# A hybrid decoder layer on one core: attention outputs split into high and low parts where they are made, and a second share of filling ahead of the last values

## The chip, the cores and the metric

The kernel runs on one core of one Trainium2 chip, as one program. The metric is the device time of one execution in microseconds (us). Engines go by their names in the profile: PE (TensorE, with PEld for its weight loads), DVE (VectorE), ACT (ScalarE), POOL (GpSimd), and SP, the engine whose queue issues nearly all transfers (DMA). Each engine works through its own instructions in order and waits on semaphores for the others.

## The reference

One layer over 1024 tokens of width 1024, all in float32: a half feed-forward, two gated attentions in parallel, a second half feed-forward, and a gated embedding. The change lies in the attentions and in the product that follows them.

```python
x = x + 0.5 * swiglu(rms_norm(x, ffn1_norm), ffn1_w_gate, ffn1_w_up, ffn1_w_down)
h = rms_norm(x, mix_norm)
fq, fk, fv, f_logit, sq, sk, sv, g_fox, g_sb = split_columns(h @ w_in)
...
y_fox = forgetting_attention(fq, fk, fv, log_f)       # 8 heads of 64, causal softmax
y_sb = stick_breaking_attention(sq, sk, sv)           # 8 heads of 64
merged = (sigmoid(g_fox) * (y_fox @ w_branch_fox)
          + sigmoid(g_sb) * (y_sb @ w_branch_sb))
x = x + merged @ w_out
x = x + 0.5 * swiglu(rms_norm(x, ffn2_norm), ffn2_w_gate, ffn2_w_up, ffn2_w_down)
x = x + sigmoid(rms_norm(x, ple_norm) @ w_ple_gate) * (p @ w_ple_proj)
```

Stick-breaking weights are `sigmoid(z[t,s])` times the product of `1 - sigmoid(z[t,j])` over the keys between s and t; the kernel makes these products with scans.

## The kernel before

**Split operands.** To multiply in float32 precision with a faster matmul type, the kernel splits an operand a into a high part (a rounded to that type, fp32r) and a low part (a minus the high part). A product is then three matmuls: high by high, high by low, low by high. `split` (lines 104 to 106) makes the two: a copy on ACT (L105), a subtraction on DVE (L106). Weights come in as RAW (L119) and are split into WH on ACT (L129) and WL on POOL (L139).

**Stages.** Feed-forward, then the projections of the attentions, then attention (about 850 to 1400 us of the profile), then the branch products, the output product, and the second feed-forward and embedding. In attention, 16 heads run one behind the other: heads 0 to 7 forgetting ("fox"), 8 to 15 stick-breaking. Two heads share a tile Y of 128 rows (64 each) by 1024 tokens, so there are eight pairs of heads, with two Y buffers.

**One step.** A head has four steps c = 0 to 3 of 256 queries each. `scores` makes the weights of a step: query-key matmuls (L1050, L1051), then for fox a sum and an exponential, for stick-breaking two sigmoids on ACT (L1058, L1059), scans on DVE (L1013, over tiles GF and RN) and multiplications on POOL (L1082). `apply` handles a step two steps later: for each pair of key blocks (`kpair` from c down to 0), PE transposes the weights (L1109), ACT copies the high part into a PT tile (L1111), DVE subtracts for the low part (L1117), and PE multiplies by the values (`values`, L1135). Values run two pairs behind the transposes; at a step's end come `values(1)`, a share of filling, and `values(0)`. The result is copied to Y by ACT (L1160) and added by DVE (L1163); the addition is issued late, at the next row of scores (`late`, `flush`).

**Filling.** PE has other work to put between: projections and stacking of later heads (L799, L807), in the last head the first branch products (L1396, gated by L1402). `fill[h]` lists the units of head h. Each call of `take`, which is what `fill` is in `scores` and `apply`, releases matmuls until their cost reaches a running target: the head's total, times the step's `share`, divided by the number of calls in that step. Some stacking units pause, and then a call gives nothing.

**The pair's way to the next product.** When the second head of a pair has its last step, SP stores the pair's Y to DRAM (`y_pairs`, L1167). In heads 14 and 15 `load_y` reads the pairs back, four at a time, into an X buffer, and `split_y` splits them with L105 and L106 on 128x1024 into H buffers, which the branch products (`branch_steps`, L1396) read as `yT[g][b]`: g is 0 for fox and 1 for stick-breaking, b is 0 for high and 1 for low. The table `Y_AT` says at which head and step the splits and loads stand. The last pair stays on the chip and is split at the end of `attention`.

**What sets the order.** The order on each engine comes from the order of the code, with a scheduler that places by dependence and by buffers: each tag (X, H, PT, Y ...) has a fixed number of them (PT has 4, H 4, X 2), and a new tile waits until the buffer's last user is done. For the stick-breaking heads `order("act", ...)` and `order("dve", ...)` pin ACT's and DVE's instructions to the order of the code. SP's transfers are one queue: one that waits holds up those behind it.

Of the kernel before, what the change touches and what calls it, by code (L numbers as in the profile page):

```python
# [10 lines left out]
F32 = mybir.dt.float32  # L11
# [7 lines left out]
P = 128  # L19
# [17 lines left out]
def tile_hybrid_decoder_layer(  # L37
# [119 lines left out]

    xd = dp.tile([S, D], F32, name="x_mid")
    pd = dp.tile([S, D], F32, name="p_proj")
    yd = dp.tile([8, P, S], F32, name="y_pairs")  # L160
    gd = dp.tile([16, P, S], F32, name="gates")
    fd = dp.tile([NH, S], F32, name="forget_sums")
    ad = [dp.tile([NF, P, 7, 512], F32, name=f"hidden_{i}") for i in range(2)]
# [930 lines left out]
    def apply(step, fill):  # L1094
# [58 lines left out]
        if c:  # L1153
            values(1)
        fill()
        values(0)
        Y = step["y"]
        hh = step["head"] % 2
# [3 lines left out]
        def add():  # L1162
            ins = nc.vector.tensor_add(ys, av[0:HD, :256], ys)  # L1163
            if not step["fox"]:
                order("dve", ins)
            if hh == 1 and c == 3 and step["last"] is False:
                nc.sync.dma_start(yd[Y["idx"]], Y["t"][:])  # L1167
        late.append(add)

    FOX_PAIRS = [2, 3, 0, 1]  # L1170
# [80 lines left out]
    def attention():  # L1251
# [26 lines left out]
        def any_bank():  # L1278
# [30 lines left out]
                s12 + g14[:1],  # L1309
                g14[1:] + s13,  # L1310
                s14 + g15[:1],
                g15[1:] + s15,
                fox_branch[:5]]

        fbs = [{} for _ in range(8)]
# [9 lines left out]
        for h in range(16):  # L1325
            fox = h < 8
            if h % 2 == 0:
                idx = fox_pairs[h // 2] if fox else 4 + (h - 8) // 2
                ys[h // 2] = {"t": slot("Y", [P, S]), "idx": idx}
            head = ys[h // 2]["idx"] % 4 * 2 + h % 2  # L1330
            v = (vf1, vf0, vs0, vs1)[h // 4]
            load_fb(h + 1)
            total = sum(u[0] for u in fill[h])
            state = [0.0, 0.0, 0]
            share = (0.27, 0.19, 0.27, 0.27)
            gens = [u[1] for u in fill[h]]

            def take(last=False):
                state[0] += total * share[state[2]] / (6, 7, 4, 5)[state[2]]
                while gens and (last or state[1] < state[0]):  # L1340
                    cost = next(gens[0], None)
                    if cost is None:
                        gens.pop(0)
                    else:
                        state[1] += cost
            for c in range(4):
                y0, y1 = Y_AT.get((h, c), ((), ()))
                split_y(*y0)
                load_y(*y1)
                step = {"fox": fox, "c": c, "head": head, "st": stacks[h], "v": v, "y": ys[h // 2], "last": h == 15, "id": 4 * h + c}  # L1350
                if fox:
                    step["fb"] = fbs[h]
                state[2] = c
                rows = scores(step, take)
                turns = apply(prev.pop(0), take) if len(prev) == 2 else iter(())
                next(rows)
                run(islice(turns, (1, 2, 1, 1)[c]))
                run(rows)
                run(turns)
                prev.append(step)  # L1360
            take(True)
# [9 lines left out]

    yT = []
    A = []
    Y_AT = {(14, 0): ((), range(4)), (14, 3): ((0, 1), (4, 5)), (15, 0): ((2, 3), (6,)), (15, 1): ((4, 5, 6), ())}

    Y_ = {}

    def load_y(*ks):
        for k in ks:
            if k == 0:  # L1380
                Y_["t"] = slot("X", [P, 4, S])
            nc.sync.dma_start(Y_["t"][:, k % 4, :], yd[k])

    def split_y(*ks):
        for k in ks:
            g, i = divmod(k, 4)
            if i == 0:
                yT.append((slot("H", [P, 4, S], F32R), slot("H", [P, 4, S], F32R)))
            hi, lo = yT[g]
            split(hi[:, i, :], lo[:, i, :], Y_["t"][:, i, :], nc.scalar, nc.vector, True)  # L1390

    def branch_steps(ps, g, m, half, w):
        i = 0
# [280 lines left out]
```

## Time and profile before

| | us |
|---|---|
| median of 3 runs | 2273.96 (2273.6 to 2276.03) |
| the profiled execution's own time | 2275.51 |
| its span in the trace | 2273.8 |
| PE busy in the span | 2241.4 |
| PE busy in 850 to 1400, of 550 us | 530.96 |
| DVE busy there | 378.09 |
| ACT busy there | 327.11 |
| POOL busy there | 336.32 |

The span runs from the first to the last instruction of the program; the execution's own time has the start and end around it as well. Busy times leave out waits and the issue of transfers. A row of the timeline reads: start, duration, engine, line, operation, output and inputs, shape, how many instructions; in brackets stands the idle time before them and what ended it.

### The profile page before, as it was taken

The page shows a single profiled execution, that of the slowest core. Times are in us where ns is not written, and L with a number is a line of the kernel's source. Part 1 is how long each engine was busy: PE and PEld are TensorE (multiplying, and loading weights), DVE is VectorE, ACT ScalarE, POOL GpSimd, SP SyncE. Part 2 cuts the span into 40 slices and gives each one's busy share as a digit, 9 for nine tenths or more (in the row PEclk, how much of TensorE's full clock was granted, in tenths as well). Part 3 has the DMA queues.
Part 4 walks back from the last instruction along what each step waited for, and adds up shares of the span by engine and source line. Part 5 has one row for each costly group of instructions (what it writes and reads, how often), then busy time and mean ns, then how long its engine had stood idle before and what let it go on. Part 6 is the DMA issues. An engine that isn't in the chain of part 4 may idle for free.

```text
span 2273.8 us, 30750 instructions
## 1 busy us (share of the span) xinstructions
PE 2241.4 (99%) x11402; PEld 1905.0 (84%) x11402; DVE 1490.0 (66%) x2296; ACT 1000.1 (44%) x1787; POOL 806.5 (35%) x803
## 2 busy tenths in 40 slices
PE   8999999999999999999999989999999999999999
PEld 6888888888888899989898878888888888888887
DVE  8845454688877326556578786789655555778753
ACT  6333333343455445565666663246333333434431
POOL 1444444300011236565467664410544444200121
PEclk9999999999999999999999999999999999999999
DMA  4232323474233343233223345732423232756132
GB/s 139 102 116 93 116 92 117 163 291 171 84 130 130 112 128 90 72 103 80 70 56 89 102 153 182 265 123 66 139 84 125 83 126 80 262 195 216 62 103 83
DMA packets 184904, 283.89 MB, mean 125 GB/s; under 512 B 27945, under 2 KB 104105, under 8 KB 184754
## 3 DMA queue, kind: packets, MB, share of 16 engines
q1 hardware_dynamic: 184752, 281.92, 37.4%
q8 instruction: 90, 1.47, 0.3%
q14 instruction: 60, 0.49, 0.1%
q10 hardware_dynamic: 2, 0.00, 0.0%
HBM read 189.83 MB, written 75.27 MB: 117 GB/s over the span
## 4 chain that ended last, share of the span: by engine, by line
PE 91%; DVE 5%; ACT 2%; issue 1%; DMA 0%; POOL 0%; SPq 0%; ACTq 0%; DVEq 0%
PE ps L556 39%; PE ps L454 21%; PE ps L799 8%; PE ps L807 4%; PE ps L1591 4%; PE ps L1396 3%; PE ps L1135 3%; PE ps L1109 2%; PE ps L506 2%; PE ps L1051 1%; PE ps L1050 1%; PE ps L956 1%; PE ps L228 1%; DVE PT L1117 1%; DVE RN L1013 1%
## 5 line engine op out<-in xcount | busy, mean ns | idle before, releaser
L454 PE MATMUL ps<-H,H 128*128 128x512 f32 x2184 | 497.7, 389 | 1.2 <-DVE X L462 1.2
L454 PEld LDWEIGHTS ps<-H,H 128*128 128x128 f32 x2184 | 409.3, 188 | 86.7 <-issue 2.0
L556 PE MATMUL ps<-H,WL 128*128 128x512 f32 x1116 | 265.0, 389 | 0.8 <-ACT WL L105 0.8
L556 PEld LDWEIGHTS ps<-H,WL 128*128 128x128 f32 x1116 | 209.4, 188 | 44.7 <-ACT WL L105 1.2
L556 PE MATMUL ps<-H,Q 128*128 128x512 f32 x612 | 146.0, 389 | 0.0
L462 DVE SCALAR_TENSOR_TENSOR X<-ps,X 128x512 f32<-128x512 f32 x168 | 109.0, 685 | 50.9 <-PE ps L454 50.9
L556 PEld LDWEIGHTS ps<-H,Q 128*128 128x128 f32 x612 | 114.9, 188 | 23.9
L556 PE MATMUL ps<-X,WL 128*128 128x512 f32 x552 | 132.6, 389 | 0.0
L1117 DVE TENSOR_TENSOR PT<-ps,PT 128x512 fp32r<-128x512 f32 (+1 forms) x160 | 100.3, 628 | 39.7 <-ACT PT L1111 38.4
L139 POOL TENSOR_TENSOR WL<-RAW,WH 128x512 fp32r<-128x512 f32 (+1 forms) x84 | 98.7, 1198 | 65.9 <-ACT WH L129 46.6
L556 PEld LDWEIGHTS ps<-X,WL 128*128 128x128 f32 x552 | 103.6, 188 | 21.5
L799 PE MATMUL ps<-WH,H 128*128 128x256 f32 x768 | 115.1, 288 | 0.6 <-ACT PT L962 0.3
L807 PE MATMUL ps<-H,WH 128*128 128x512 f32 x384 | 114.3, 408 | 0.6 <-ACT PT L926 0.6
L1135 PE MATMUL ps<-PT,X 128*128 128x256 f32 (+1 forms) x640 | 105.0, 290 | 9.5 <-DVE PT L1117 5.4
L219 POOL TENSOR_SCALAR ss<-ss 128x1 f32<-128x1 f32 x28 | 8.4, 299 | 297.9 <-ACT WL L215 232.8
L1111 ACT CAST PT<-ps 128x512 fp32r<-128x512 f32 (+1 forms) x160 | 87.6, 548 | 55.8 <-PE ps L1109 55.2
L1135 PEld LDWEIGHTS ps<-PT,X 128*128 128x128 f32 x640 | 91.8, 193 | 22.3 <-DVE PT L1117 11.3
L556 PE MATMUL ps<-H,PT 128*128 128x512 f32 x456 | 108.9, 389 | 0.0
L799 PEld LDWEIGHTS ps<-WH,H 128*128 128x128 f32 x768 | 101.0, 190 | 1.7 <-ACT PT L962 0.5
L556 PEld LDWEIGHTS ps<-H,PT 128*128 128x128 f32 x456 | 85.5, 188 | 17.8
L355 POOL TENSOR_TENSOR PT<-GF,RN 128x512 f32<-128x512 f32 x20 | 33.6, 1680 | 184.7 <-DVE GF L710 184.7
L1063 POOL TENSOR_TENSOR T<-T,l 128x128 f32<-128x128 f32 (+3 forms) x64 | 73.5, 1150 | 72.1 <-DVE l L1062 70.2
(431 smaller groups left out, 4899.1 us busy)
## 6 DMA issues: line engine op xcount, KB each, us to landing
hidden<-PT SPq DMA_DIRECT2D x40, 512.0 KB, 3.1
WH<-in_ffn_w_gate_dram SPq DMA_DIRECT2D x38, 512.0 KB, 5.5
Q<-hidden SPq DMA_DIRECT2D x24, 512.0 KB, 6.4
hidden<-RN SPq DMA_DIRECT2D x22, 512.0 KB, 2.6
KH<-in_ffn_w_up_dram SPq DMA_DIRECT2D x20, 512.0 KB, 6.4
KL<-in_ffn_w_up_dram SPq DMA_DIRECT2D x20, 512.0 KB, 6.9
T<-in_ffn_w_down_dram SPq DMA_DIRECT2D x20, 512.0 KB, 7.5
X<-in_x_dram SPq DMA_DIRECT2D x16, 512.0 KB, 9.8
```

The costliest lines, as they stand in the source:

```text
L139: ins = eng_lo.tensor_sub(lo[part], raw[part], f(hi[part]))
L454: pe(nc.tensor.matmul(groups[g][t][:], act[:, a, k, t * P:(t + 1) * P], wt[:, b, k, :], start=(fresh and n == 0), stop=(i in (6, 1, 4) and ...
L462: nc.vector.scalar_tensor_tensor(xs, groups[g][t][:], scale, xs, ALU.mult, ALU.add)
L556: pe(nc.tensor.matmul(ps[:], hl[:, a, k, :], rhs(m, b, k), start=(first and i == 0), stop=(final and i == 11), skip_group_check=True))
L799: pe(nc.tensor.matmul(ps[:, :n], hT[t // 4](a, k)[:, (t % 4) * P:(t % 4 + 1) * P], w[k // 4][b][:, k % 4, :n], start=(i == 0), stop=(i == ...
L807: pe(nc.tensor.matmul(ps[:], w[a][:, k, :], hT[half](b, k), start=(i == 0), stop=(i == 23)))
L1063: nc.gpsimd.tensor_mul(T[:, :n], T[:, :n], l[:].broadcast_to([P, n]))
L1111: high = nc.scalar.copy(pt[:, 0, :width], ps[:, :width])
L1117: ins = nc.vector.tensor_sub(pt[:, 1, :width], ps[:, :width], f(pt[:, 0, :width]))
L1135: pe(nc.tensor.matmul(o, lh, r, start=(kpair == c and i == 0), stop=(kpair == 0 and i == 3)))
L1396: pe(nc.tensor.matmul(ps[:], w[a][:, k, :], yT[g][b][:, k, half * 512:half * 512 + 512], start=(i == 0), stop=(i == 11)))
L1591: pe(nc.tensor.matmul(ps, hT[t // 4](a, k)[:, (t % 4) * P:(t % 4 + 1) * P], pl["w"][d, k // 2][b][:, k % 2, cs], start=(i == 0), stop=(i = ...
```

## The change

The tile `yd` in DRAM holds each pair twice, high and low. Each half of a pair (512 tokens, done after steps 1 and 3 of the second head) is split behind its addition: the high part goes into a PT tile by ACT, the low part is written over Y by DVE, and SP stores both. The loads in heads 13 to 15 bring the parts straight into the tiles that the products read; `split_y` is gone. `values(0)` has two calls of filling ahead of it, and the divisors of the shares follow. The units of head 14 are put in another order, with the last gate unit ahead of most of the last stacking.

```diff
-    yd = dp.tile([8, P, S], F32, name="y_pairs")
+    yd = dp.tile([8, 2, P, S], F32, name="y_pairs")
...
         if c:
             values(1)
         fill()
+        fill()
         values(0)
...
             ins = nc.vector.tensor_add(ys, av[0:HD, :256], ys)
             if not step["fox"]:
                 order("dve", ins)
-            if hh == 1 and c == 3 and step["last"] is False:
-                nc.sync.dma_start(yd[Y["idx"]], Y["t"][:])
+            if hh == 1 and c % 2 and not step["last"]:
+                cs = slice(c // 2 * 512, c // 2 * 512 + 512)
+                hi = slot("PT", [P, 512], F32R)
+                a = nc.scalar.copy(hi[:], Y["t"][:, cs])
+                b = nc.vector.tensor_sub(Y["t"][:, cs].bitcast(F32R), Y["t"][:, cs], f(hi[:]))
+                if not step["fox"]:
+                    order("act", a)
+                    order("dve", b)
+                nc.sync.dma_start(yd[Y["idx"], 0][:, cs], f(hi[:]))
+                nc.sync.dma_start(yd[Y["idx"], 1][:, cs], Y["t"][:, cs])
...
-                g15[1:] + s15,
+                s15[:1] + g15[1:] + s15[1:],
...
-                state[0] += total * share[state[2]] / (6, 7, 4, 5)[state[2]]
+                state[0] += total * share[state[2]] / (7, 8, 5, 6)[state[2]]
...
-                y0, y1 = Y_AT.get((h, c), ((), ()))
-                split_y(*y0)
-                load_y(*y1)
+                load_y(*Y_AT.get((h, c), ()))
...
-    Y_AT = {(14, 0): ((), range(4)), (14, 3): ((0, 1), (4, 5)), (15, 0): ((2, 3), (6,)), (15, 1): ((4, 5, 6), ())}
-
-    Y_ = {}
-
-    def load_y(*ks):
+    Y_AT = {(13, 0): (0, 0, range(4)), (14, 2): (0, 1, range(4)), (15, 0): (1, 0, range(4, 6)), (15, 1): (1, 1, range(4, 6)), (15, 2): (1, 0, (6,)), (15, 3): (1, 1, (6,))}
+
+    def load_y(g=None, b=None, ks=()):
+        if g is None:
+            return
+        if len(yT) == g:
+            yT.append([None, None])
+        if yT[g][b] is None:
+            yT[g][b] = slot("H" if g or b else "X", [P, 4, S], F32R)
         for k in ks:
-            if k == 0:
-                Y_["t"] = slot("X", [P, 4, S])
-            nc.sync.dma_start(Y_["t"][:, k % 4, :], yd[k])
-
-    def split_y(*ks):
-        for k in ks:
-            g, i = divmod(k, 4)
-            if i == 0:
-                yT.append((slot("H", [P, 4, S], F32R), slot("H", [P, 4, S], F32R)))
-            hi, lo = yT[g]
-            split(hi[:, i, :], lo[:, i, :], Y_["t"][:, i, :], nc.scalar, nc.vector, True)
+            nc.sync.dma_start(f(yT[g][b][:, k % 4, :]), yd[k, b])
```

In the changed kernel the lines from 1157 on are numbered one higher, then more: the addition is L1164, the new copy L1170, the new subtraction L1171, the stores L1175 and L1176, the loads L1391, the branch products L1397 and their gating L1403.

How the instructions move is shown at three places. First DVE's order in head 15, from the first gated branch product (into Q) to the next low part (PT) of `apply`, before:

```order
L1402 TENSOR_TENSOR Q_12688<-Q_12688,ps_12689 128x512
L106 TENSOR_TENSOR H_12771<-X_12300,H_12770 128x1024 x3
L1013 TENSOR_SCALAR GF_12681<-GF_12681,mask_sb 128x127
L1163 TENSOR_TENSOR Y_12299<-ps_12700,Y_12299 64x256
L1013 TENSOR_SCALAR RN_12716<-RN_12716,mask_sb 128x128
L1013 TENSOR_SCALAR RN_12716<-RN_12716 128x127
L1117 TENSOR_TENSOR PT_12795<-ps_12791,PT_12795 128x384
```

and with the change:

```order
L1403 TENSOR_TENSOR Q_12746<-Q_12746,ps_12747 128x512
L1117 TENSOR_TENSOR PT_12800<-ps_12795,PT_12800 128x512
L1013 TENSOR_SCALAR GF_12739<-GF_12739,mask_sb 128x127
L1164 TENSOR_TENSOR Y_12358<-ps_12758,Y_12358 64x256
L1013 TENSOR_SCALAR RN_12773<-RN_12773,mask_sb 128x128
L1013 TENSOR_SCALAR RN_12773<-RN_12773 128x127
L1117 TENSOR_TENSOR PT_12848<-ps_12844,PT_12848 128x384
```

Three splits of y pairs stood between the gating and the next scans and low parts; now none do.

Second DVE's order where the first half of the pair of heads 10 and 11 is complete (Y is the pair's tile, GF and RN are scans of the running step), before:

```order
L1013 TENSOR_SCALAR RN_11528<-RN_11528 128x256
L1163 TENSOR_TENSOR Y_10800<-ps_11509,Y_10800 64x256
L1013 TENSOR_SCALAR GF_11493<-GF_11493 128x256
L1117 TENSOR_TENSOR PT_11600<-ps_11596,PT_11600 128x384
L1013 TENSOR_SCALAR RN_11528<-RN_11528 128x256
```

and with the change:

```order
L1013 TENSOR_SCALAR RN_11572<-RN_11572 128x256
L1164 TENSOR_TENSOR Y_10836<-ps_11553,Y_10836 64x256
L1171 TENSOR_TENSOR Y_10836<-Y_10836,PT_11627 128x512
L1013 TENSOR_SCALAR GF_11538<-GF_11538 128x256
L1117 TENSOR_TENSOR PT_11649<-ps_11645,PT_11649 128x384
L1013 TENSOR_SCALAR RN_11572<-RN_11572 128x256
```

The subtraction stands directly behind the addition whose result it needs, and reads the PT tile that ACT fills in between; the scans and the low part stand behind it. The other thirteen halves look the same.

Third PE's order at the end of a step of head 14 (the values of `kpair` 1, branch products, the values of `kpair` 0, the next scores), before:

```order
L1135 MATMUL ps_12700<-PT_12731,X_10264 128x256 x4
L1396 MATMUL ps_12751<-H_12571,WL_12435 128x512
L1396 MATMUL ps_12751<-H_12571,WH_12433 128x512
L1396 MATMUL ps_12751<-H_12572,WH_12433 128x512
L1135 MATMUL ps_12700<-PT_12743,X_10264 128x256 x4
L1050 MATMUL ps_12783<-KH_12439,Q_12438 128x384
```

and with the change:

```order
L1135 MATMUL ps_12758<-PT_12787,X_10300 128x256 x4
L1397 MATMUL ps_12817<-X_11989,WH_12379 128x512
L1397 MATMUL ps_12817<-H_12562,WH_12379 128x512
L1397 MATMUL ps_12817<-X_11989,WL_12381 128x512
L1397 MATMUL ps_12817<-X_11989,WH_12379 128x512
L1397 MATMUL ps_12817<-H_12562,WH_12379 128x512
L1135 MATMUL ps_12758<-PT_12800,X_10300 128x256 x4
L1050 MATMUL ps_12836<-KH_12385,Q_12384 128x384
```

Five matmuls of filling stand between the two groups of values instead of three; the high part of y is now read from an X tile. In the first part of the stick-breaking heads two become four or three become six.

## Prediction

> **What bounds the kernel now.** I read first the shares of the whole page, then the chain that ended last.
>
> ```profile
> span 2273.8 us, 30750 instructions
> PE 2241.4 (99%) x11402; PEld 1905.0 (84%) x11402; DVE 1490.0 (66%) x2296; ACT 1000.1 (44%) x1787; POOL 806.5 (35%) x803
> PE 91%; DVE 5%; ACT 2%; issue 1%; DMA 0%; POOL 0%; SPq 0%; ACTq 0%; DVEq 0%
> ```
>
> TensorE is busy 99% of the span, so a change that leaves its matmuls alone can win only what PE loses: idle time and time at a low clock. Outside PE the chain holds DVE first. The change touches the attention stage alone (about 850 to 1400 us), so next come PE's waits there (the columns are the total, the number of waits and the longest, in us).
>
> ```profile
> PE ps L1135 <- DVE PT L1117: 5.4, 13, 0.8
> PE ps L1109 <- DVE PT L1117: 4.3, 2, 3.6
> PE ps L1135 <- ACT PT L1111: 3.5, 4, 1.2
> PE ps L1109 <- POOL WL L139: 2.0, 1, 2.0
> ```
>
> L1135 are the value matmuls, L1109 the transposes ahead of them. Where the long waits lie, the table by stretches shows: the stretch and its length, then PE, PEld, DVE, ACT and POOL busy, PE's granted clock, the DMA share and GB/s.
>
> ```profile
> 1220.00:1260.00 40.00, 39.83 (x236) 34.29 (x234) 33.86 (x55) 25.55 (x55) 27.76 (x42) 1.00 0.30 67
> 1324.00:1339.00 15.00, 14.47 (x78) 12.17 (x77) 10.85 (x19) 13.49 (x27) 6.80 (x10) 1.00 0.51 151
> 1339.00:1362.00 23.00, 17.20 (x92) 14.62 (x92) 22.34 (x31) 11.61 (x23) 18.70 (x23) 0.85 0.66 212
> 1362.00:1380.00 18.00, 17.69 (x98) 14.97 (x97) 14.95 (x25) 11.99 (x28) 10.45 (x17) 1.00 0.49 160
> ```
>
> Attention is covered almost everywhere (39.83 of 40), except in 1339 to 1362, where the last head starts: PE idles 5.80 us, its clock falls to 0.85, and DVE is busy 22.34 of 23. There DVE is the bound. The chain of waits of that stretch alone, by line, and the rows of both engines name the work:
>
> ```profile
> by line: DVE H L106 31.2%; DVE GF L1013 12.1%; PE ps L1135 11.6%; DVE RN L1013 11.5%; PE ps L1109 8.4%; PE ps L1396 7.6%; DVE PT L1117 7.0%; issue 6.6%; DVE Y L1163 2.7%; DVE KL L882 2.6%; DVEq L106 0.1%
> 1338.61 2.83 DVE L106 TENSOR_TENSOR H<-X,H 128x1024 fp32r<-128x1024 f32 x2
> 1348.99 4.43 DVE L106 TENSOR_TENSOR H<-X,H 128x1024 fp32r<-128x1024 f32 x3
> 1345.16 0.63 PE L1109 MATMUL ps<-identf,T 128*128 128x128 f32 x4 [2.01 <-POOL WL L139]
> 1355.69 1.09 PE L1109 MATMUL ps<-identf,T 128*128 128x128 f32 x4 [3.58 <-DVE PT L1117]
> 1359.57 1.78 PE L1135 MATMUL ps<-PT,X 128*128 128x256 f32 x8
> 1361.19 0.40 PE L1396 MATMUL ps<-H,WL 128*128 128x512 f32 x1
> 1251.69 1.09 PE L1135 MATMUL ps<-PT,X 128*128 128x256 f32 x8
> ```
>
> The two blocks of L106 are `split_y`: the low parts of y pairs, 2.83 + 4.43 = 7.26 us of DVE in a row order that puts the scans (L1013) and L1117 of the running head behind them. PE then waits 2.01 and 3.58 us. Behind the second gap eight matmuls take 1.78 us, against 1.09 for the same eight at 1251.69, and four transposes 1.09 against 0.63 at 1345.16: 1.6 to 1.7 times as long, and the rows of L1396 are short again (0.40) from 1361.19 on. Of these 5.5 us (1355.69 to 1361.19) some 2.2 are lost to the clock. The stretch loses 5.8 + 2.2 = 8.0 us.
>
> **Term A, the removed splits: -6.5 us.** Seven copies on ACT and seven L106 on DVE leave the end of attention; the loads now bring finished operands. PE alone could win 8.0. DVE's remaining work sets another limit: 22.34 - 7.26 = 15.1 us, so the stretch can't be under 15.1 (a gain of 7.9), even with DVE busy all the time. In 1220 to 1260 DVE's share beside a full PE is 33.86/40 = 85%; at that share 15.1 us need 17.7, a gain of 5.3. I take 6.5, between the two, since DVE has room before and behind (10.85 of 15, 14.95 of 18) and may work ahead. Low end: only the longest gap goes, -3.6. Late next is POOL (18.70 of 23 busy), which multiplies the scans' results.
>
> The clock needs a word. Gaps much shorter than 3.58 also came before a slow stretch:
>
> ```profile
> 1100.66 0.39 PE L1135 MATMUL ps<-PT,X 128*128 128x256 f32 x1 [1.17 <-ACT PT L1111]
> 1101.39 0.81 PE L1135 MATMUL ps<-PT,X 128*128 128x256 f32 x3 [0.34 <-DVE PT L1117]
> 1100.00:1140.00 40.00, 38.65 (x209) 33.10 (x210) 24.74 (x62) 23.14 (x50) 17.64 (x23) 0.96 0.34 80
> ```
>
> After 1.17 and 0.34 us the 40-us stretch has a clock of 0.96, 1.6 us of full speed lost. So a leftover gap of over a microsecond can keep part of the 2.2; this is inside the ends of A. The Trainium skill ("TensorE: Matmul & The Clock Gate", section "HAM oscillation — how this bites in real kernels") states that PE falls back to the low clock after idle gaps of over about 3.4 us. By that rule, any rest of the 3.58-us gap below 3.4 would give back all the lost clock and A would lean to 7.9; the row at 1101 speaks against so high a threshold, and I keep 6.5.
>
> **Term B, the second share ahead of `values(0)`: -3.0 us.** `values(0)` waits for the last L1117 or L1111 of its step. Two more matmuls (three or more in the larger steps) of projection work, 0.2 us and more each, now lie between. Of L1135's waits (5.4 + 3.5 us) I sorted each by its place in PE's order. Ten lie at `values(0)` where the new order has more filling, the first, the largest and the last of them head the rows below; the ten sum to 2.99 us. Two that stay follow.
>
> ```profile
> 984.99 0.39 PE L1135 MATMUL ps<-PT,X 128*128 128x256 f32 x1 [0.18 <-DVE PT L1117]
> 1199.36 0.39 PE L1135 MATMUL ps<-PT,X 128*128 128x256 f32 x1 [0.81 <-DVE PT L1117]
> 1375.18 0.39 PE L1135 MATMUL ps<-PT,X 128*128 128x256 f32 x1 [0.31 <-DVE PT L1117]
> 909.87 0.38 PE L1135 MATMUL ps<-PT,X 128*128 128x256 f32 x1 [1.18 <-ACT PT L1111]
> 1261.00 0.39 PE L1135 MATMUL ps<-PT,X 128*128 128x256 f32 x1 [0.75 <-DVE PT L1117]
> ```
>
> The wait at 909.87 stays: there both shares are empty, because the stacking units pause. The one at 1261.00 stands at `values(1)`, ahead of the new share. The sum of work is the same, so each other share shrinks by an eighth to a fifth; PE is at 39.83 of 40 with them, and thinner ones may open gaps elsewhere. Ends: -6 (the waits at `values(1)` shrink too, and the clock loss at 1101) and +2.
>
> **Term C, the 14 new splits: +3.2 us.** Seven pairs, two halves each: on ACT a 128x512 copy (new line 1170), on DVE a 128x512 subtraction (1171) directly behind the pair's addition (L1163, now 1164). No such split stands in the middle of attention; the last pair's, of the same shape, does at its end. Its ACT row and its DVE row:
>
> ```profile
> L105 ACT CAST H<-Y 128x512 fp32r<-128x512 f32 x2 | 1.2, 624 | 2.2 <-DVE Y L1163 2.2
> L106 DVE TENSOR_TENSOR H<-Y,H x2: 685/686/686, 1379.1 to 1396.5; 128x512 fp32r<-128x512 f32 x2
> 1246.84 0.42 DVE L1163 TENSOR_TENSOR Y<-ps,Y 64x256 f32<-64x256 f32 x1
> 1250.50 0.69 DVE L1117 TENSOR_TENSOR PT<-ps,PT 128x512 fp32r<-128x512 f32 x1 [0.20 <-ACT PT L1111]
> 1324.74 0.42 DVE L1163 TENSOR_TENSOR Y<-ps,Y 64x256 f32<-64x256 f32 x1 [1.11 <-ACT Y L1160]
> 1326.73 0.56 DVE L1117 TENSOR_TENSOR PT<-ps,PT 128x384 fp32r<-128x384 f32 x1 [1.10 <-ACT PT L1111]
> ```
>
> DVE issues the addition, waits for ACT's copy of its result (0.62), then subtracts (0.69): about 1.35 us with the two hand-overs, during which everything behind it, scans and L1117, stands still. At 1246.84 (the first half of heads 10 and 11) DVE has only 0.20 idle before the L1117 at 1250.50, which would end at 1251.19 + 1.15 = 1252.34; PE's values at 1251.69 would be 0.65 late. Three such halves in stick-breaking heads: 2.0. At 1324.74 (the second half of heads 12 and 13) the 1.10 idle ahead of L1117 takes up all but 0.25, and part of that lies under filling: 3 x 0.13 = 0.4. The eight halves in forgetting heads meet a DVE that is less loaded (24.74 of 40 in 1100 to 1140): 0.1 each, 0.8. Ends: 0 (all hidden) and 14 x 1.35 = 18.9 (nothing hidden).
>
> **Term D, buffers and queues: +0.5 us.** The high half takes one of the four PT buffers and holds it until its store has landed. Rows: stores of that size, the store of a pair, its issue, the fourth user of PT behind 1246.84, and SP's worst wait; and the first reader of x_mid.
>
> ```profile
> gates<-PT SPq DMA_DIRECT2D x8, 256.0 KB, 3.1
> 1325.18 0.34 SPq L1167 DMA_DIRECT2D y_pairs<-Y  x1
> 1255.18 0.48 ACT L1111 CAST PT<-ps 128x384 fp32r<-128x384 f32 x1
> SPq L119 <- ACT WH L129: 88.5, 12, 23.7
> L460 DVE TENSOR_TENSOR X<-ps,X x28: 681/684/692, 1475.7 to 1534.4; 128x512 f32<-128x512 f32 x28
> ```
>
> SP issued the pair's store 0.44 us behind the addition at 1324.74. A copy done by 1247.9, stored by 1248.4 and landed 3.1 us later frees its buffer at 1251.5, 3.7 us ahead of 1255.18. It fails only where the store stands in SP's queue behind a weight load that itself waits (up to 23.7 us), hence 0.5, with ends 0 and +5. The 28 stores and 14 loads in place of 7 and 7 are 28 more issues of 0.34 us, 9.5 us of SP's queue over the stage; behind them stand weight loads and the stacking transfers of the next head. SP waits far longer than that for other things (88.5 us in the row of L119 alone), so they fit in; without that slack they would cost up to their 9.5 us, which C's upper end holds. The reload of x_mid comes some 40 us later, since its X buffer now holds operands; the additions that read it begin at 1475.7, which leaves 60 us of cover.
>
> **Sum.** -6.5 - 3.0 + 3.2 + 0.5 = -5.8 us. The profiled execution took 2275.51 (span 2273.8 plus 1.7 around it); it is 1.55 above the median of the runs, 2273.96. So 2269.7 for the profiled one and **2268.2** for the median.
>
> **Rivals.**
> - *DVE's round trip reaches PE (slower).* If PE waits for all 1.35 us at each split, C is 18.9 and the sum -6.5 - 3.0 + 0.5 + 18.9 = +9.9: 2283.9. For it: DVE at 85% in stick-breaking heads, and values that follow L1117 by half a microsecond. Against it: 39.83 of 40 there, so PE's filling does take up DVE's jitter. It decides from 9.0/14 = 0.64 us per split.
> - *The tail's wait passes to POOL.* Only the 3.58 gap goes: -3.6 - 3.0 + 3.2 + 0.5 = -2.9: 2271.1. For it: the 2.01 gap was released by POOL. Against: POOL itself waits for scans behind L106.
> - *The second share is given back.* B = +2: sum -0.8, 2273.2; the change would then not do what it says for PE. For it: fillings shrink at every other place. Against: waits at those places are few.
> - *The new subtractions hold POOL.* POOL's multiplication of equal shape took:
>
> ```profile
> 1348.28 0.64 POOL L1082 TENSOR_TENSOR T<-T,RN 128x256 f32<-128x256 f32 x1
> 1349.48 1.62 POOL L1082 TENSOR_TENSOR T<-T,RN 128x256 f32<-128x256 f32 x1
> ```
>
> The second ran under the L106 at 1348.99, 0.98 us longer. The new subtraction reads two operands from SBUF as L106 did; 14 x 0.98 = 13.7 if all reaches PE: sum +7.9, 2281.9. Against: POOL is 27.76 of 40 busy beside the full PE, and the same rule frees POOL in the tail. The Trainium skill ("SBUF — State Buffer", section "Who interferes with whom") states that a DVE instruction with two SBUF inputs contends with a GpSimd instruction that reads SBUF; the pair of rows agrees.
>
> **How the numbers follow.** Chances: forecast 0.56, round trip 0.17, POOL in the tail 0.12, POOL held 0.09, share given back 0.06. A median within 0.2% (4.5 us) of 2273.96 can't be told from it. The forecast's own range, 2263 to 2273, lies with 0.47 below 2269.4 and 0.09 above; the tail rival gives 0.05 faster, 0.07 same; the given-back share 0.04 same, 0.02 slower; the round trip 0.02 same, 0.15 slower; POOL held 0.09 slower. Together faster 0.52, same 0.22, slower 0.26. The range reaches from A's and B's better ends, about 2260, to 2282, which takes in most of both slower rivals.
>
> **What would show it.** A: no L106 H<-X, PE over 21 of 23 us around the start of the last head at a clock near 1.00. B: L1135's waits on L1117 down from 5.4 to about 3, those on L1111 nearly the same. C: gaps of 0.3 to 0.7 us at L1135 or L1109 behind the first-half splits of stick-breaking heads only, 14 waits of DVE for line 1170 of about 0.65. D: no wait of L1111 for a DMA. Wrong I would be if PE's gaps behind the splits exceed 0.7 us each, if the clock falls in new places, or if the tail keeps a gap of over 2 us.

## The result, and the profile after

| | us |
|---|---|
| before, median of 15 runs | 2275.27 (2273.6 to 2276.36) |
| with the change, median of 15 runs | 2270.18 (2268.49 to 2272.18) |
| ratio | 0.9979, 95% interval 0.9971 to 0.9987 |
| profiled execution with the change, its span | 2270.58, 2268.9 |

The ratio is 4.8 us of 2275 (3.0 to 6.6); the forecast was 5.8, and its 2268.2 stands 2.0 under the median, inside its range.

The page of the changed kernel, the same three lines as before (span; busy time and share of each engine; the chain that ended last):

```profile
span 2268.9 us, 30821 instructions
PE 2238.0 (99%) x11402; PEld 1902.5 (84%) x11402; DVE 1484.3 (65%) x2303; ACT 997.9 (44%) x1794; POOL 801.7 (35%) x803
PE 92%; DVE 4%; ACT 2%; issue 1%; DMA 0%; POOL 0%; SPq 0%; ACTq 0%; DVEq 0%; POOLq 0%
```

The number of matmuls is the same. PE's waits in 850 to 1400 of the changed kernel:

```profile
PE ps L1135 <- DVE PT L1117: 5.5, 12, 1.3
PE ps L1109 <- DVE PT L1117: 3.2, 5, 0.9
PE ps L1109 <- DVE l L1062: 2.9, 2, 2.0
PE ps L1135 <- ACT PT L1111: 2.1, 3, 1.6
```

The wait of 3.6 at L1109 and the one for L139 are gone. In their place L1109 has two longer waits for L1062, the reciprocal of a forgetting row, and the value matmuls wait for L1117 as long as before (5.5 against 5.4). The stretch tables show both sides:

```profile
1220.00:1260.00 40.00, 39.39 (x231) 33.91 (x230) 33.35 (x55) 25.56 (x56) 26.73 (x42) 1.00 0.35 84
1342.10:1357.70 15.60, 14.80 (x92) 12.43 (x92) 14.37 (x25) 8.05 (x19) 13.03 (x20) 1.00 0.71 210
```

From the first branch product (L1396, now L1397) to ACT's last copy into Y for head 14 (L1160, now L1161) the kernel before took 1339.38 to 1362.3; now it is 1342.1 to 1357.7. The same 92 matmuls need 15.6 us instead of 22.9, at full clock. Up to there, however, the changed kernel is later: it reaches the last head at 1342.1, not at 1339.4.

To see where, the spans are cut at 16 marks: the fourth ACT copy into Y of each head. The table holds the length of each stretch (head 0 from the first matmul of L454 on; "end" up to the matmuls of L454 behind attention) minus that of the kernel before.

```
head          0     1     2     3     4     5     6     7     8     9    10    11    12    13    14    15   end   sum
change      1.9  -0.7   0.5   0.1  -0.5  -0.1   0.7   0.0   0.0   0.0   0.0   0.6   0.2   0.3  -8.1   1.3  -1.4  -5.1
```

So 8.1 us are won in one stretch, and 3.0 are lost over heads 0 to 13, 1.9 of them in head 0, where no split falls. The experiments divide these among the parts. Most such differences repeat to 0.1 us from kernel to kernel; a stretch that falls into a low clock does not, and each table is one execution.

### The profile page after: what moved, and what is told of

Same layout as the page of the kernel before. It is cut to its first block, busy times and chain, and to the rows that moved or that the text cites. A ratio compares the mean times of both kernels' runs of the same rounds, so it can differ in the third digit from the quotient of the medians.

```text
span 2268.9 us, 30821 instructions
## 1 busy us (share of the span) xinstructions
PE 2238.0 (99%) x11402; PEld 1902.5 (84%) x11402; DVE 1484.3 (65%) x2303; ACT 997.9 (44%) x1794; POOL 801.7 (35%) x803
## 4 chain that ended last, share of the span: by engine, by line
PE 92%; DVE 4%; ACT 2%; issue 1%; DMA 0%; POOL 0%; SPq 0%; ACTq 0%; DVEq 0%; POOLq 0%
PE ps L556 39%; PE ps L454 21%; PE ps L799 7%; PE ps L807 5%; PE ps L1592 4%; PE ps L1397 4%; PE ps L1135 3%; PE ps L506 2%; PE ps L1109 2%; PE ps L1051 1%; PE ps L1050 1%; PE ps L956 1%; PE ps L228 1%; DVE PT L1117 1%; DVE RN L1013 1%
## 5 line engine op out<-in xcount | busy, mean ns | idle before, releaser
L454 PE MATMUL ps<-H,H 128*128 128x512 f32 x2184 | 497.7, 389 | 1.2 <-DVE X L462 1.2
L454 PEld LDWEIGHTS ps<-H,H 128*128 128x128 f32 x2184 | 409.4, 188 | 86.6 <-issue 2.0
L139 POOL TENSOR_TENSOR WL<-RAW,WH 128x512 fp32r<-128x512 f32 (+1 forms) x84 | 98.6, 1196 | 68.0 <-ACT WH L129 42.5
L1117 DVE TENSOR_TENSOR PT<-ps,PT 128x512 fp32r<-128x512 f32 (+1 forms) x160 | 100.1, 628 | 31.1 <-ACT PT L1111 30.2
L1135 PE MATMUL ps<-PT,X 128*128 128x256 f32 (+1 forms) x640 | 102.8, 287 | 8.2 <-DVE PT L1117 5.5
L1111 ACT CAST PT<-ps 128x512 fp32r<-128x512 f32 (+1 forms) x160 | 87.2, 549 | 47.9 <-PE ps L1109 43.9
L1135 PEld LDWEIGHTS ps<-PT,X 128*128 128x128 f32 x640 | 90.7, 191 | 18.6 <-DVE PT L1117 10.2
```

Source lines behind the costliest of these rows:

```text
L139: ins = eng_lo.tensor_sub(lo[part], raw[part], f(hi[part]))
L454: pe(nc.tensor.matmul(groups[g][t][:], act[:, a, k, t * P:(t + 1) * P], wt[:, b, k, :], start=(fresh and n == 0), stop=(i in (6, 1, 4) and ...
L1111: high = nc.scalar.copy(pt[:, 0, :width], ps[:, :width])
L1117: ins = nc.vector.tensor_sub(pt[:, 1, :width], ps[:, :width], f(pt[:, 0, :width]))
L1135: pe(nc.tensor.matmul(o, lh, r, start=(kpair == c and i == 0), stop=(kpair == 0 and i == 3)))
```

## The experiments

Each kernel ran beside the kernel before on the same chip. Times in us below are (1 - ratio) x 2275 under that kernel; intervals are those of the ratio.

The granted clock listed with each run tells more than a median. The 15 runs of the change took 2268.49 to 2268.97 us at a clock of 1.000 (3 runs), 2269.97 to 2270.64 at 0.999 (9) and 2271.52 to 2272.18 at 0.998 (3). Such a step of 1.6 us is about what one short stretch at half clock costs (last section), so a median also tells how often a kernel fell into one. The table takes runs of like clock: the median of each kernel's runs at 1.000 (for kernels 1, 3 and 5, which have none, at 0.999), minus that of the change at the same clock. The groups are small, the clock is rounded and the kernels ran on several chips, so it is a reading beside the medians and not a test.

```
kernel               1     3     4     5     6     7     8     9    10    11    12
runs                 2     5     1     3     2     1     1     2     3     7     4
us to the change  -0.5  -3.4  -0.9  -2.6  -1.9  -2.0  -0.9  -3.0  -4.3   0.9  -4.1
```

**1. One share.** The change without its second share.

```diff
         fill()
-        fill()
         values(0)
...
-                state[0] += total * share[state[2]] / (7, 8, 5, 6)[state[2]]
+                state[0] += total * share[state[2]] / (6, 7, 4, 5)[state[2]]
```

> The change without its second share (one call of filling ahead of the last values, the old divisors): splits moved, nothing else. Theory (the forecast's terms: A -6.5, B -3.0, C +3.2, D +0.5): A + C + D = -2.8, so 2.8 us under the kernel before (about 2272.5) and 2.3 over the change (2270.2). Rival, that the second share gains nothing and the end of attention more: about -6 to -7 against before (2268.5 to 2269.5), no slower than the change.

Measured: 2270.72, ratio 0.9986 (0.9977 to 0.9994), 3.2 us under. The theory's 2.8 fits the number, not its parts: with the parts as kernels 2 and 3 measure them it would be 4.8. The difference to the change (1.6) is smaller than what the two intervals leave open, and the clock can account for it: 9 of these 11 runs are at 0.998, 3 of 15 of the change's, and at like clock this kernel is 0.5 under the change, not over it.

**2. The share alone.** The opposite edit, on the kernel before.

> The kernel before with the second share alone (two calls of filling and the new divisors, splits as before). Theory: B = -3.0, so 2272.3. Rival, that thinner shares give back what the second one covers: within 1 us of before or up to 2 us over it (2275 to 2277).

Measured: 2273.9, ratio 1.0 (0.9991 to 1.0008). The rival holds: the second share alone gains nothing in time. PE's waits in 850 to 1400 of this kernel say why:

```profile
PE ps L1109 <- DVE PT L1117: 6.4, 4, 3.0
PE ps L1135 <- DVE PT L1117: 5.7, 13, 1.2
PE ps L1109 <- DVE l L1062: 2.4, 2, 1.5
PE ps L1135 <- ACT PT L1111: 2.2, 3, 1.6
```

L1135's waits are 7.9 in all against 8.9, but all of PE's waits in that view sum to 19.2 against 18.4. Those ahead of the last values shrank, but the ones at the values of `kpair` 1, ahead of the new share, grew, since the shares before them are thinner. Two rows of the timeline, whose waits were 0.75 (at 1261.00) and 0.34 (at 1322.33) before:

```profile
1258.77 0.50 PE L1135 MATMUL ps<-PT,X 128*128 128x256 f32 x2 [1.18 <-DVE PT L1117]
1320.30 0.39 PE L1135 MATMUL ps<-PT,X 128*128 128x256 f32 x1 [0.81 <-DVE PT L1117]
```

And L1109's waits for L1062 grew from 1.3 to 2.4. The lengths by head, cut as above and minus the kernel before, show the giving and the taking:

```
head          0     1     2     3     4     5     6     7     8     9    10    11    12    13    14    15   end   sum
kernel 2    1.9  -1.1   0.5  -0.4  -0.6  -0.7  -0.3  -0.9   0.0  -0.8  -0.1   0.1   0.1   0.0   0.3   1.3  -1.4  -2.0
```

Heads 6 and 7 hold a stretch at half clock in the kernel before and none here, which is 1.7 of the 2.0.

**3. No split in the middle.** The changed kernel with Y itself stored as both parts.

```diff
-                hi = slot("PT", [P, 512], F32R)
-                a = nc.scalar.copy(hi[:], Y["t"][:, cs])
-                b = nc.vector.tensor_sub(Y["t"][:, cs].bitcast(F32R), Y["t"][:, cs], f(hi[:]))
...
-                nc.sync.dma_start(yd[Y["idx"], 0][:, cs], f(hi[:]))
+                nc.sync.dma_start(yd[Y["idx"], 0][:, cs], Y["t"][:, cs])
```

> The change without the 14 copies and 14 subtractions: Y itself is stored as both parts (this leaves the split of seven pairs out of the computation); loads, PE's order and both shares as in the change. Theory: C + D are gone but for the stores, so 3.2 us under the change, about 2267. Rival 1, splits are hidden: as the change (2270.2). Rival 2, each split costs its whole round trip: 14 x 1.35 = 19 us under the change.

Measured: 2266.79, ratio 0.9968 (0.9955 to 0.998), 7.3 us under. So the 14 splits with their PT buffers cost 7.3 - 4.8 = 2.5 us; the forecast had 3.7. At like clock they cost 3.4. The lengths by head, same cut as above, minus kernel 3 (the rows of later kernels are used below):

```
head               0     1     2     3     4     5     6     7     8     9    10    11    12    13    14    15   sum
change           0.0   0.5   0.0   0.5   0.0   0.5   0.5  -0.1   0.0   0.8   0.0   0.4   0.1   0.4   0.0   0.0   3.6
kernel 4         0.0   0.5   0.0   2.0   0.0   0.7   0.6  -0.3   0.0   0.3   0.0   0.1   0.0   0.0   0.3  -0.1   4.2
kernel 5         0.0   0.2   0.3   2.0   0.0   0.5   0.5  -0.7   0.0   0.0   0.0  -0.1   0.0  -0.1   0.0   0.0   2.4
kernel 6         0.0   0.5   0.0   0.0   0.0   0.2   1.0  -0.8   0.0   0.6   0.0   0.1   0.0  -0.1   0.0   0.0   1.4
kernel 9        -0.1   1.1   0.0   0.3  -0.1   0.7  -1.8  -0.4   0.0   0.0  -0.1  -0.1   0.0  -0.1  -0.2  -0.2  -1.1
kernel 10       -0.1   0.0   0.0   0.2  -0.1  -0.3  -0.7  -0.6   0.0   0.0  -0.1  -0.1  -0.2  -0.1  -0.2  -0.2  -2.5
kernel 11        0.0   1.1   0.0   0.3   0.0   1.1  -1.7  -0.4  -0.1   0.8   0.0   0.4   0.0   0.4   0.2  -0.1   2.1
```

Every stretch from head 1 to head 14 of the change holds one split: the odd ones a first half (behind step 1 of the pair's second head), the even ones a second half (behind step 3, issued late and so in the next head's stretch). First halves cost 0.3 to 0.8 us, second halves 0.1 at most. Heads 6 and 7 have to be taken together: in kernels 3 to 6 and in the change a stretch at half clock lies at the mark between them and is shared out differently, which leaves 0.3 for the first half in head 7 (PE's idle time grew there alone, from 0.42 to 0.89); in kernels 9 to 11 it is missing, which is 1.7 of the difference there. Of the 3.6, 1.9 lie in heads 1 to 8 (splits of forgetting heads) and 1.7 in heads 9 to 14 (splits of stick-breaking heads).

**4. The subtraction one place later**, so that DVE doesn't stand and wait for ACT's copy.

```diff
-        while late:
-            late.pop(0)()
+        todo = late[:]
+        late.clear()
+        for fn in todo:
+            fn()
...
+                def sub():
+                    b = nc.vector.tensor_sub(Y["t"][:, cs].bitcast(F32R), Y["t"][:, cs], f(hi[:]))
+                    if not step["fox"]:
+                        order("dve", b)
+                    nc.sync.dma_start(yd[Y["idx"], 1][:, cs], Y["t"][:, cs])
+                late.append(sub)
```

> The change with each new subtraction issued one place later (after the next low part on DVE instead of directly behind the addition), so that DVE does not wait for ACT's copy; all else, PE's order too, as in the change. Theory (half of what a split costs is DVE's wait of 0.65 us for ACT): 1 to 1.5 us under the change, about 2268.9. Rival, only the 0.69 us of DVE work counts: as the change. Rival, the PT buffer held longer stalls ACT: 1 to 3 us over the change.

Measured: 2269.36, ratio 0.9979 (0.997 to 0.9988): as the change. The wait itself did go. With the change, DVE's waits for the copy read:

```profile
DVE Y L1171 <- ACT PT L1170: 5.4, 8, 0.9
```

and in this kernel, where the copy is L1172 and the subtraction L1178:

```profile
DVE Y L1178 <- ACT PT L1172: 0.8, 2, 0.4
```

Heads 9, 11 and 13 came down from 0.8, 0.4 and 0.4 to 0.3, 0.1 and 0.0 over kernel 3, which is the theory's 1.2. But head 3 stood at 2.0 instead of 0.5, in a stretch at a low clock (below), and in the median nothing was left that this measurement can tell. At like clock the kernel is 0.9 under the change.

**5 and 6. Each half of the split by itself.** Kernel 5 keeps the copy, the PT buffer and both stores; kernel 6 keeps only a subtraction of the same size. The line of kernel 6:

```diff
+                b = nc.vector.tensor_sub(Y["t"][:, cs].bitcast(F32R), Y["t"][:, cs], Y["t"][:, cs])
```

> The change with ACT's copy, the PT buffer and both stores, but without the 14 subtractions on DVE (this leaves the low part out: Y itself is stored in its place). With neither, the kernel ran 7.2 us under the one before, with both 4.8 under. Theory (what a split costs PE is DVE's time): as with neither, about 7 under. Rival, that ACT's copy or the held PT buffer is the price: as the change, 4.8 under.

> The change with a subtraction of the same size on DVE (Y minus Y), without ACT's copy and without the PT buffer (this leaves the split out of the computation). Theory: as the change, 4.8 under the kernel before, since 0.69 us of DVE stays at each of the 14 places. Rival (copy or PT buffer): about 7 under.

Measured: the copy alone 2269.04, ratio 0.9973 (0.9963 to 0.9983), 6.1 under; the subtraction alone 2267.29, ratio 0.9966 (0.9954 to 0.9978), 7.7 under, by the median no slower than with neither. The theory that DVE's own 0.69 us is the whole price falls. But the subtraction is not free: in the table it keeps 0.5 at head 1 and 0.6 at head 9, and its trace is 1.4 longer than kernel 3's. At like clock the copy alone costs 0.8 over kernel 3, the subtraction alone about 1.5 (2266.66 at 1.000, under the change by 1.9 where kernel 3 is under it by 3.4), both together 3.4.

The trace of the change shows what the copy does in a forgetting head. ACT's rows about 990 and the PE row behind them, the change first:

```profile
989.64 0.40 ACT L1061 ACTIVATE T<-T,m 128x128 f32<-128x128 f32 x1
990.04 0.60 ACT L1170 CAST PT<-Y 128x512 fp32r<-128x512 f32 x1
990.66 0.69 ACT L884 ACTIVATE KH<-ps,gqk 128x512 fp32r<-128x512 f32 x1
991.25 0.47 ACT L1111 CAST PT<-ps 128x384 fp32r<-128x384 f32 x1
992.75 0.30 PE L1109 MATMUL ps<-identf,T 128*128 128x128 f32 x1 [2.04 <-DVE l L1062]
```

and the same rows without splits (kernel 3):

```profile
988.90 0.40 ACT L1061 ACTIVATE T<-T,m 128x128 f32<-128x128 f32 x1
989.42 0.69 ACT L884 ACTIVATE KH<-ps,gqk 128x512 fp32r<-128x512 f32 x1
990.01 0.47 ACT L1111 CAST PT<-ps 128x384 fp32r<-128x384 f32 x1
991.51 0.30 PE L1109 MATMUL ps<-identf,T 128*128 128x128 f32 x1 [1.52 <-DVE l L1062]
```

From the exponential (L1061) to L1111 it is 1.61 us with the copy and 1.11 without, and PE's wait behind it is 2.04 against 1.52: the 0.5 us of head 3. DVE's subtraction, which waits for the copy and runs 0.69 from 990.67 on, ends there with ACT's L884 (991.35), so DVE's next instruction (L885, at 991.39) is held by both.

**7. High parts first.** The change with the values of a pair of key blocks in another order.

```diff
                 mm = [mm[0], mm[2], mm[3], mm[1]]
+            else:
+                mm = [mm[0], mm[2], mm[1], mm[3]]
```

> The change with the four value matmuls of a pair of key blocks in the order high, high, low, low instead of high, low, high, low, so that a second one is ready while PE waits for the low part. In the change's trace 15 waits stand behind the first of the four, 5.9 us in all; one matmul is 0.11 us. Theory: up to 15 x 0.11 = 1.6 us under the change. Rival, that a wait for DVE comes back at the next place: as the change.

Measured: 2267.84, ratio 0.9968 (0.9955 to 0.998), 7.3 under, 2.5 under the change (the theory's top is 1.6; the intervals overlap) and 2.0 at like clock. L1135's waits for L1117 (here L1137) fell from 5.5:

```profile
PE ps L1137 <- DVE PT L1117: 4.0, 11, 1.1
```

**8. The share at the other place**, ahead of `values(1)` instead of ahead of `values(0)`.

```diff
         if c:
+            fill()
             values(1)
-        fill()
         fill()
         values(0)
...
-                state[0] += total * share[state[2]] / (7, 8, 5, 6)[state[2]]
+                state[0] += total * share[state[2]] / (7, 8, 4, 6)[state[2]]
```

> The change with its second share ahead of the values of kpair 1 instead of ahead of the last ones (for the one-pair step it stays out). In the traces the longest waits of L1135 on L1117 in the last step of a head (1.30 at 1263.87, 0.71 at 1325.78) stand at kpair 1, ahead of the new share. Theory (the share stands behind the wait that it should cover): 1 to 2 us under the change. Rival, that DVE is the limit of the step's end, and the wait passes to the last values: as the change or up to 1 over it.

Measured: 2269.93, ratio 0.9978 (0.9969 to 0.9987): as the change. A gain of a microsecond isn't ruled out: at like clock this kernel is 0.9 under the change, but 6 of its 11 runs are at 0.998, and its trace has a second stretch at half clock, in head 3.

**9 to 11. Splits off the busy engines.** Kernels 9 and 10 take the order of kernel 7, the late subtraction of kernel 4 in stick-breaking heads only, and give both instructions of the split in forgetting heads to DVE (9) or POOL (10). Kernel 11 is the change with just the copy on DVE in forgetting heads. From kernel 10:

```diff
+                if step["fox"]:
+                    nc.gpsimd.tensor_copy(hi[:], Y["t"][:, cs])
+                    nc.gpsimd.tensor_sub(Y["t"][:, cs].bitcast(F32R), Y["t"][:, cs], f(hi[:]))
+                    nc.sync.dma_start(yd[Y["idx"], 0][:, cs], f(hi[:]))
+                    nc.sync.dma_start(yd[Y["idx"], 1][:, cs], Y["t"][:, cs])
+                    return
```

> The change with three edits: the value matmuls in the order high, high, low, low; the late subtraction in stick-breaking heads only; in forgetting heads both instructions of the split on DVE, so that ACT has none. Theory (the price of a split is ACT's 0.6 in front of other ACT work in forgetting heads, 0.5 each at heads 1, 3, 5 and 6, and DVE's wait for ACT in stick-breaking heads, 0.8, 0.4 and 0.4): 2.2 for the order of the values, 2.0 and 1.2 for the splits, so about 5 us under the change, 10 under the kernel before (ratio 0.9956). Rival, that DVE's 0.69 more in forgetting heads costs as much as ACT's: 3.4 under the change (0.9964).

> As e9_combined_dve, but in forgetting heads both instructions of the split on POOL. Theory: neither ACT nor DVE waits, 5 us under the change (0.9956). Rival, that POOL's multiplications behind it (L1063) are held for over 2 us each and reach PE's transposes: at or above the change (0.998 or more).

> The change with one edit: in forgetting heads DVE makes the high part instead of ACT. Theory (in forgetting heads the price of a split is ACT's copy, which stands ahead of exponentials and of copies for PE): the 0.5 us each at heads 1, 3, 5 and 6 go, 2 us under the change (ratio 0.9970), and the stretches of those heads in the trace come back to those without splits. Rival (DVE's time is the price): as the change or up to 2 over it.

Measured: kernel 9 2265.59, ratio 0.9962 (0.9948 to 0.9975); kernel 10 2264.42, ratio 0.9956 (0.9944 to 0.9969), 10.0 under the kernel before; kernel 11 2269.57, ratio 0.9977 (0.9968 to 0.9986), as the change. That kernel 10 hit the expected 0.9956 to the digit is in part luck with the clock: 3 of its 5 runs are at 1.000, and at like clock it is 4.3 under the change instead of 5. In the table, heads 1, 3 and 5 stand at 1.1, 0.3 and 1.1 with the copy on DVE (11), at 0.0, 0.2 and -0.3 with the split on POOL (10), and heads 9, 11 and 13 at 0.0, -0.1 and -0.1 (10). So "ACT's copy is the price" was too narrow: in forgetting heads the split costs on ACT and on DVE alike. On POOL it costs PE nothing that the trace shows, though the subtraction takes longer there (1.29 us; the copy takes 0.61, as on ACT; rows of kernel 10):

```profile
L1175 POOL CAST PT<-Y x8: 609/612/812, 913.3 to 1134.6; 128x512 fp32r<-128x512 f32 x8
L1176 POOL TENSOR_TENSOR Y<-Y,PT x8: 1268/1292/1378, 914.3 to 1135.6; 128x512 fp32r<-128x512 f32 x8
```

**12. One share again**, on kernel 10.

> As e10_combined_pool, with one call of filling ahead of the last values and the old divisors: what the second share is worth where splits no longer disturb (e10 ran 10 us under the kernel before, ratio 0.9956). By the forecast's term B (3.0): 7 under before (0.9969). By the traces (ten waits covered, others grown, B about 1.5): 8.5 under (0.9963). Rival, the second share is worth nothing: 10 under (0.9956).

Measured: 2264.52, ratio 0.9952 (0.9939 to 0.9966), 10.9 under; kernel 10 is 10.0 under, and 0.2 ahead of this one at like clock. With splits out of the way, too, the second share is worth nothing that can be told.

## Why the prediction was right, and where it was not

By the timed kernels the parts are: A, the splits taken from the end of attention, kernel 3 against kernel 2, both with two shares: 7.3 won (this holds the new order of the units of head 14 and the new loads too; no run takes them apart). B, the second share: 0.0 (kernel 2), 1.6 won (change against kernel 1), 0.9 lost (kernel 12 against 10). C and D, the new splits with buffers: 2.5 lost. With B at 0, -7.3 + 2.5 = -4.8, which is the measured total by the way it is built; the forecast had -6.5 - 3.0 + 3.2 + 0.5 = -5.8. Each difference of two timed kernels is uncertain by some 3 us; only A is clear of that. That the total came within 1.0 us is partly luck: the 3.0 of B did not come, and A was 0.8 larger, C with D 1.2 smaller than forecast.

- **What bounds it: right.** PE, at full cover but for the start of the last head, where DVE's two blocks of L106 were the bound. With them gone, the stretch went from 22.9 to 15.6 us.
- **Term A: right, a little small (7.3 timed, 8.1 in the stretch of head 14).** 6.5 was put between a DVE share of 85% and of 100% in what remains. The row 1342.10:1357.70 has DVE at 14.37 of 15.60, which is 92%, with PE at 14.80. The rival that POOL takes over fell: POOL is busy 13.03 of 15.60, and no long wait of PE stands there. The clock there was 1.00. The loss to the clock in the old stretch was larger than the 2.2 that the prediction read from its rows: cut finely, PE was busy 5.38 us at a clock of 0.50, which is 2.7 lost.

```profile
1354.24:1361.07 6.83, 5.38 (x23) 5.12 (x24) 6.79 (x12) 1.17 (x2) 4.58 (x9) 0.50 0.56 184
```

- **Term B: did not come, and the step that failed is "the ten sum to 2.99 us", taken as won.** The prediction named the other end itself (each other share shrinks by an eighth to a fifth) and put it at nothing in the sum; that other end took back all of the gain. Nor were all ten covered: of the three shown, the largest (0.81) went, but 0.18 and 0.31 stayed (in the change 0.17 at 986.10 and 0.32 at 1370.58), while the wait of 1.18 at 909.87, which was to stay, went. In kernel 2 L1135's waits went from 8.9 to 7.9 only, and those of L1109 for L1062 from 1.3 to 2.4. The sign named for B came out the other way round: in the change L1135's waits for L1117 stayed (5.4, now 5.5) and those for L1111 fell (3.5, now 2.1). It was the rival "the second share is given back", to which 0.06 was given, with B at 0 instead of +2. That the shares give no gain is shown by kernels 1, 2 and 12; that it is the thinning and not the new order as such is read from the rows that grew, and was not tried apart. In single profiled executions two of the three pairs put the second share about 2 us ahead and one 0.8 behind. In both of the two, 1.7 is a stretch at half clock that only the kernel with one share fell into (the kernel before from 1101.65 on, kernel 12 from 911.70 on).
- **Term C: right in size (3.6 in the trace and 3.4 at like clock, 2.5 timed, all with D; 3.2 and 0.5 forecast), wrong in its division.** The prediction had first halves of stick-breaking heads at 0.65 each, second halves at 0.13, and every half of a forgetting head at 0.1. First halves cost 0.8, 0.4 and 0.4 in stick-breaking heads and 0.3 to 0.5 in the four forgetting ones; second halves cost 0.1 at most in either. So the first halves were named rightly for stick-breaking heads, and the step that failed is the 0.1 for forgetting heads: the prediction looked at DVE's load alone, and there the split stands ahead of ACT's or DVE's work for the next transposes. In stick-breaking heads the round trip is most of the price: without the wait (kernel 6) 0.6 of 1.6 is left, all in head 9, and with the late subtraction (kernel 4) 0.4. The 14 waits of about 0.65 were 8, of 0.68 on average (0.34 to 0.88).
- **Term D: small, as said.** "No wait of L1111 for a DMA" was wrong for one of 2.5 us behind the store of a gate (`gates<-PT`); the stores of the new high parts held up only one L863 by 0.8, and one addition, at 1334.7, waited 1.9, by the profile for the store of a low part out of Y:

```profile
ACT PT L1111 <- DMA gates<-PT: 2.5, 1, 2.5
DVE Y L1164 <- DMA y_pairs<-Y: 1.9, 1, 1.9
ACT PT L863 <- DMA y_pairs<-PT: 0.8, 1, 0.8
```

- **The rival "round trip reaches PE": it did, at the three first halves of stick-breaking heads, for 1.6 us in all**, not for 1.35 at each of 14 places.
- **The rival "the new subtractions hold POOL": fell.** Kernel 6 has all 14 of them, and its trace is 1.4 us longer than that of kernel 3 without, whatever the cause, not 13.7. Holding showed on the other side: the subtraction itself took 1.48 in head 9 and 1.55 in head 10 of the change instead of 0.69. In head 10 this cost PE nothing; head 9 lost 0.8, heads 11 and 13 (at 0.69) 0.4, and whether the holding is part of that is not shown.

```profile
L1171 DVE TENSOR_TENSOR Y<-Y,PT x14: 681/693/1553, 914.9 to 1329.5; 128x512 fp32r<-128x512 f32 x14
```

The Trainium skill ("SBUF — State Buffer", section "Who interferes with whom") has it that the order of issue decides which of the two blocks. This agrees with a subtraction that is the one to wait, but no run here tells which POOL instruction held it.

## What to carry to other kernels

A share of filling that is moved is taken from somewhere: before counting the waits that it covers, look for the nearest waits that its old places cover. Work taken off a stretch that one engine bounds was worth nearly its whole time here, and the same work spread over a covered stage cost only where it stood ahead of what the bounding engine needs next; there a less loaded engine (POOL), at twice the time for the subtraction, beat a busier one. Before a difference of one or two microseconds is read as the work of an edit, compare the granted clock of the runs. Where two operands come from two engines, issue first the matmuls that need the earlier one.

## What was not expected of the hardware

The clock falls after gaps of about the same length in one kernel and not in another. Kernels 4 and 5 and the change have the same order on PE and a wait of about 2.0 us at the same transposes in head 3: 2.04 in the change, 2.02 in kernel 4. The four us behind it (stretch, then PE, PEld, DVE, ACT and POOL busy, the clock, DMA share, GB/s), in the change:

```profile
993.00:997.00 4.00, 4.00 (x36) 4.00 (x35) 1.11 (x2) 0.98 (x3) 1.25 (x3) 1.00 0.97 335
```

and in kernel 4:

```profile
992.22 0.45 PE L1111 MATMUL ps<-identf,T 128*128 128x128 f32 x1 [2.02 <-DVE l L1064]
993.00:997.00 4.00, 4.00 (x26) 4.00 (x25) 0.69 (x1) 0.58 (x1) 0.87 (x2) 0.68 0.84 290
```

In the four us 26 matmuls passed instead of 36, which is most of the 1.5 us that head 3 lost in the table. The threshold of about 3.4 us that the Trainium skill states ("TensorE: Matmul & The Clock Gate", section "HAM oscillation — how this bites in real kernels") does not hold here: one gap of 2.02 us was enough, one of 2.04 was not.

What differs is where the gap lies. Wherever the clock falls between 850 and 1400 us in the traces, it stands at 0.50 for 3.41 us (at the end of attention in the kernel before and kernel 2 for twice that) and at 1.00 on both sides, so one such period costs up to 1.7 us. In one trace the falls lie whole multiples of 3.413 us apart: 112.64 in kernels 4, 5 and 8 (33 times), 252.59 in the kernel before (74 times). Cut into periods of that length, counted back from a fall, kernel 4 has PE idle for 1.98 of 3.41 us in the period ahead of its fall:

```profile
988.77:992.18 3.41, 1.43 (x13) 1.22 (x11) 2.69 (x9) 3.36 (x9) 1.13 (x2) 1.00 0.35 60
992.18:995.59 3.41, 3.37 (x16) 3.40 (x17) 0.77 (x2) 0.58 (x1) 1.49 (x3) 0.50 1.02 353
```

In the change the same gap lies across two periods, with 0.74 and 1.53 us idle, and no fall follows:

```profile
987.81:991.22 3.41, 2.67 (x22) 2.29 (x20) 2.54 (x8) 3.33 (x7) 2.62 (x3) 1.00 0.01 3
991.22:994.63 3.41, 1.88 (x16) 1.91 (x17) 2.12 (x5) 1.47 (x5) 1.50 (x3) 1.00 0.96 263
```

Over all traces, PE idled 1.40 to 2.12 us in the periods ahead of the falls, and at most 1.64 in one that no fall followed (kernels 9 and 10). So a gap of 1 to 2 us costs up to 1.7 us more than its length when it happens to lie within one period. This is read from the traces; no run moved a gap by itself. Nor does a clock of 1.00 mean that a gap was removed: in 1100 to 1140 the clock is 0.96 before and in the change and 1.00 in kernel 10, yet PE's wait there is 1.64 us both in the change (first row) and in kernel 10, where L1139 is the line of the values:

```profile
1102.51 0.39 PE L1135 MATMUL ps<-PT,X 128*128 128x256 f32 x1 [1.64 <-ACT PT L1111]
1100.28 0.51 PE L1139 MATMUL ps<-PT,X 128*128 128x256 f32 x2 [1.64 <-ACT PT L1113]
1100.00:1140.00 40.00, 38.80 (x223) 33.41 (x224) 26.73 (x62) 23.38 (x49) 22.86 (x29) 1.00 0.39 98
```
